# The last three memory key tiles as products of rounded fp32 parts

## The chip, the cores and the metric

The kernel runs on one core of a Trainium2 chip. The core has a matrix engine (PE, with its weight loads shown as PEld), a vector engine (DVE), a scalar engine (ACT), GpSimd (POOL) and a queue that issues transfers (SP). Each engine works off its own instructions in the order in which they were written. The metric is the device time of one execution in microseconds (us); the profile describes one such execution.

## The reference

One step of a decoder layer over 1024 prompt tokens and 8 new tokens, model width 1024. It begins, as far as this change goes, with the keys and values of 256 memory tokens:

```python
def rms_norm(x, g):
    xf = x.astype(jnp.float32)
    y = xf * lax.rsqrt(jnp.mean(xf * xf, axis=-1, keepdims=True) + EPS)
    return (y * g.astype(jnp.float32)).astype(x.dtype)

def memory_kv(mem, g, w_mk, w_mv):
    m = rms_norm(mem, g)
    k = jnp.einsum('bmd,de->bme', m, w_mk)      # 256 x 1024, an output
    v = jnp.einsum('bmd,de->bme', m, w_mv)      # 256 x 1024, an output
...
h = rms_norm(x, g_mix)
z = jnp.einsum('btd,de->bte', h, w_in)          # the first dense products
```

Behind it come a short convolution, an indexer with top-k, sparse attention, attention over the memory and a feed-forward block, which this change doesn't touch.

## The kernel before

Activations lie transposed in SBUF: x is eight tiles `xs[k]` of 128 channels by 1032 tokens, the memory is two tiles `mg[a]` that hold four groups of 128 channels by 256 tokens each. A product of high accuracy is made from parts: a value is split into a rounded high part (ACT, `AF.Copy` to the type fp32r) and a rest (DVE or POOL, a subtraction), and PE computes high x high, high x low and low x high. Weights arrive as units of 128x1024 (`W`): `load_to` issues the transfer on SP, `split_to` splits a unit (ACT at L163, the subtraction on DVE here, L165), `take(8)` hands out the eight blocks of a split unit after making sure that the next ones are loaded and split, and `take_raw` hands out an unsplit unit.

The first 70 us run in program order, with no scheduler:

- Loads are issued in a row on SP: memory and unit 0, then units 1 and 2, x0 and x1, unit 3, x2 and x3, unit 4, x4 and x5, unit 5, x6 and x7, then units 6 to 10.
- Units 0 to 7 are the memory key weights, one for each of the eight key tiles `j`. A key tile is eight products of 128x256 in plain fp32, of `w` and `mg` (L733); the trace shows two records for each product. DVE evicts tile `j` at L708 (`evict_mk`).
- Between the tiles stands the norm of x: ACT squares the tiles x0 to x7 (L697, at j = 1 to 5) and DVE adds them up into `xacc` (L703, one round later). After tile 6, PE sums `xacc` over the partitions (`rstd_sum`, L442), DVE and ACT make the inverse root and a diagonal of it (`rstd_chain`, L446 to L454), and unit 8 is split. After tile 7, PE spreads the root over all rows (`rstd_rows`, L461), copied out at L462.
- Units 8 to 15 are the memory value weights (L781), made from parts. Beside each unit DVE also scales one tile of x (`xnorm`, L719) and subtracts for its split (`split_sb`, L502; the copy on ACT is L499).
- Then the dense products over x begin (L480, `dense`), whose first weight is unit 16.

Buffers come from a ring of 49 slots (`S.get`, `S.put`), oldest first.

Of the kernel before, what the change touches and what calls it, by code (L numbers as in the profile page):

```python
# [110 lines left out]


MIX_UNITS = 24
PE_STEP = "pe"


# [82 lines left out]
class UnitWeights:  # L199


    def __init__(self, nc, slots, ws):
        self.nc, self.slots, self.ws = nc, slots, ws
        self.n = MIX_UNITS
        self.raw, self.hl = {}, {}
# [61 lines left out]
class Background:  # L267
# [15 lines left out]
    def step(self, g):  # L283
        try:
# [3 lines left out]
            return None  # L288
        if c == PE_STEP:
            self.blocked.append(g)  # L290
# [34 lines left out]
def build(tc, A):  # L325
# [15 lines left out]
    PS = psum.tile([128, 8, 512], F32, name="PS")  # L341
    S = Slots(main)
    W = Weights(nc, S, A["ws"])
    W.limit = 21
    bg = Background()
    V, ACT, G, PE = nc.vector, nc.scalar, nc.gpsimd, nc.tensor
    later = []

    def flush():
        for f in later:  # L350
            f()
        later.clear()
# [25 lines left out]
    def load_mem(a, hf):  # L378
        c = slice(512 * hf, 512 * hf + 512)
        nc.sync.dma_start(memr[a][0][:, c], A["memT"][:, 4 * a + 2 * hf:4 * a + 2 * hf + 2, :].rearrange("p k m -> p (k m)"))  # L380
# [8 lines left out]
    for hf in range(2):  # L389
        c = slice(512 * hf, 512 * hf + 512)  # L390
        load_mem(0, hf)
        nc.sync.dma_start(w0[0][:, c], A["ws"][0][:, c])
    W.loaded, W.split = 1, 8
    load_mem(1, 0)
    load_mem(1, 1)
    for w, x in ((3, 2), (4, 4), (5, 6), (6, 8)):
# [43 lines left out]
    def rstd_sum(sq, gp, ng):  # L440
        for g in range(ng):
            PE.matmul(PS[0:gp, 6, g:g + 1], sq[:, g * gp:(g + 1) * gp], ones[:, 0:1], start=True, stop=True)  # L442

    def rstd_chain(gp, ng, src=None):
        v, r, t = sv[0:gp, 0:ng], sr[0:gp, 0:ng], stt[0:gp, 0:ng]
        V.tensor_scalar(v, PS[0:gp, 6, 0:ng] if src is None else src, 1.0 / 1024, EPS, op0=ALU.mult, op1=ALU.add)  # L446
        ACT.activation(t, v, AF.Sqrt)
        V.reciprocal(r, t)
        V.tensor_tensor(t, r, r, op=ALU.mult)
        V.scalar_tensor_tensor(t, t, -0.5, v, op0=ALU.mult, op1=ALU.mult)  # L450
        V.scalar_tensor_tensor(r, t, 1.5, r, op0=ALU.add, op1=ALU.mult)
        dg = S.get()
        d = dg[0][0:gp, 0:ng * gp].rearrange("p (g n) -> p g n", n=gp)
        V.tensor_tensor(d, ident[0:gp, 0:gp].unsqueeze(1).to_broadcast([gp, ng, gp]),  # L454
                        r.unsqueeze(2).to_broadcast([gp, ng, gp]), op=ALU.mult)
        return dg

    def rstd_rows(dg, gp, dst, width, chunk):
        for i, c in enumerate(range(0, width, chunk)):
            b = 6 + i % 2  # L460
            PE.matmul(PS[:, b, :chunk], ones[0:gp, :], dg[0][0:gp, c:c + chunk], start=True, stop=True)  # L461
            (V.tensor_copy if i % 2 == 0 else ACT.copy)(dst[:, c:c + chunk], PS[:, b, :chunk])  # L462
        S.put(dg)
# [33 lines left out]
    def split_sb(src, scale=None, lo=None, width=T):  # L497
        h, l = S.get(F32R), S.get(F32R)
        ACT.activation(h[0][:, :width], src[0][:, :width], AF.Copy, scale=1.0 if scale is None else scale)  # L499
        hf = h[0].bitcast(F32)[:, :width]  # L500
        if scale is None:
            (lo or G).tensor_tensor(l[0][:, :width], src[0][:, :width], hf, op=ALU.subtract)  # L502
        else:
            V.scalar_tensor_tensor(l[0][:, :width], src[0][:, :width], scale, hf, op0=ALU.mult, op1=ALU.subtract)
        return h, l
# [172 lines left out]
    mg = [S.get(), S.get()]  # L678
    W.lo_engines = [V]
    for k in range(8):  # L680
        a, c = k // 4, (k % 4) * 256
# [13 lines left out]
    def x_square(k):  # L695
        xsq[k] = S.get()
        ACT.activation(xsq[k][0][:, :T], xs[k][0][:, :T], AF.Square)  # L697

    def x_accum(k):
        if k == 0:  # L700
            xacc[0] = xsq[0]
        else:
            V.tensor_tensor(xacc[0][0][:, :T], xacc[0][0][:, :T], xsq[k][0][:, :T], op=ALU.add)  # L703
            S.put(xsq[k])

    def evict_mk(j):
        dst = mstage[j // 4][0][:, (j % 4) * 256:(j % 4) * 256 + 256]
        V.tensor_tensor(dst, PS[:, j % 6, :256], mR[0][:, :256], op=ALU.mult)  # L708
        if j % 4 == 3:
            a = j // 4  # L710
            store(mkT[4 * a:4 * a + 4].rearrange("k p m -> p k m"),
                  mstage[a][0][:, :1024].rearrange("p (k m) -> p k m", m=256), mstage[a])

    dgm = dgx = None
    mh, ml = [], []
# [6 lines left out]
        h.append(split_sb(xs[k], lo=V))  # L722

    for j in range(8):
        w = W.take_raw()
        flush()
        if j == 0:
            for a in range(2):
                ACT.activation(msq[a][0][:, :1024], memr[a][0][:, :1024], AF.Square)
                S.put(memr[a])  # L730
        for k in range(8):
            a, c = k // 4, (k % 4) * 256
            PE.matmul(PS[:, j % 6, :256], w[0][:, 128 * k:128 * k + 128], mg[a][0][:, c:c + 256], start=k == 0, stop=k == 7)  # L733
        S.put(w)
        if j == 0:
            V.tensor_tensor(msq[0][0][:, :1024], msq[0][0][:, :1024], msq[1][0][:, :1024], op=ALU.add)
            V.tensor_tensor(msq[0][0][:, :512], msq[0][0][:, :512], msq[0][0][:, 512:1024], op=ALU.add)
            V.tensor_tensor(msq[0][0][:, :256], msq[0][0][:, :256], msq[0][0][:, 256:512], op=ALU.add)
            S.put(msq[1])
        if j == 1:  # L740
            rstd_sum(msq[0][0], 128, 2)
            dgm = rstd_chain(128, 2)
            V.tensor_copy(mrs, sr[:, 0:2])
            S.put(msq[0])
        if j == 2:
            rstd_rows(dgm, 128, mR[0], 256, 256)
            for a in range(2):
                hl = split_sb(mg[a], lo=V, width=1024)
                mh.append(hl[0])
                ml.append(hl[1])  # L750
        for k in X_SQUARE.get(j, ()):
            x_square(k)
        for k in X_SQUARE.get(j - 1, ()):
            x_accum(k)
        if j >= 2:
            for q in ([0, 1, 2] if j == 2 else [j]):
                evict_mk(q)
        if j == 6:
            rstd_sum(xacc[0][0], 86, 12)
            dgx = rstd_chain(86, 12)  # L760
            S.put(xacc[0])
            xR = S.get()
            W.split_to(9)
        if j == 7:
            rstd_rows(dgx, 86, xR[0], T, CH)
    for t in mg:
# [2 lines left out]
    for hv in range(2):  # L769
        for kp in range(4):  # L770
            blocks = W.take(8)
            flush()
            u = W.cur - 1
            for p in range(3):
                for kk in range(2):
                    k = 2 * kp + kk
                    a, c = k // 4, (k % 4) * 256
                    x = ml if p == 1 else mh
                    w = (W.L if p == 2 else W.H)[u][0][:, kk * 512:kk * 512 + 512]
                    for m in range(2):  # L780
                        PE.matmul(PS[:, 2 - 2 * hv + m, :], x[a][0][:, c + 128 * m:c + 128 * m + 128], w,  # L781
                                  start=(k == 0 and p == 0), stop=(k == 7 and p == 2))
# [88 lines left out]
    for n, t in enumerate((7, 6, 5, 4, 3, 2, 1, 0, 8)):  # L871
        c0 = NS + 128 * t if t < 8 else 0
        b = n % 6
        for k in range(8):
# [3 lines left out]
            for p, (x, w) in enumerate(((hh, wh), (hl, wh), (hh, wl))):  # L878
                PE.matmul(PS[:, b, :260], x[0][:, c0:c0 + 128], w[0][:, ws], start=(k == 0 and p == 0),
                          stop=(k == 7 and p == 2))  # L880
# [621 lines left out]
    mg = []  # L1502
# [111 lines left out]
    def mem_sample(hd):  # L1614
# [4 lines left out]
        for x in range(2):  # L1619
            V.tensor_copy(rep[:, 128 * x:128 * x + 128].rearrange("p (b r) -> p b r", r=16),  # L1620
                          qm_s[:, 2 * hd + x, :].unsqueeze(2).to_broadcast([128, NS, 16]))
        yield PE_STEP
        for x in range(2):
# [13 lines left out]
        yield None  # L1637
        yield PE_STEP
        PE.matmul(P, sel128, p, start=True, stop=True)
# [6 lines left out]
        yield None  # L1646
        yield PE_STEP
        for x in range(2):
# [215 lines left out]
    UW.n = A["wu"].shape[0]  # L1864
    UW.load(MIX_UNITS)
    for f in FF_DIRECT:
# [10 lines left out]
        if f == 0:  # L1877
            UW.sums(MIX_UNITS)
            UW.high(MIX_UNITS, "U")
            UW.low(MIX_UNITS, "U")  # L1880
        else:
            UW.high(MIX_UNITS, "V")
            UW.low(MIX_UNITS, "V")
# [92 lines left out]
    blocks = W.take(8 * n)  # L1976
# [72 lines left out]
    for c, cn in enumerate(CW):  # L2049
# [8 lines left out]
        for o in seq:  # L2058
# [5 lines left out]
            if prev is not None:  # L2064
# [4 lines left out]
                if o >= FIN_AT + 2:  # L2069
                    z = o - FIN_AT - 2  # L2070
                    w = 6 - FIN_AT
# [92 lines left out]
```

## Time and profile before

| | |
|---|---|
| median of three runs | 2075.16 us (2074.70 to 2077.28) |
| the profiled execution | 2075.18 us, of which the span is 2073.4 us |
| PE busy | 2037.3 us, 98% of the span |
| DVE busy | 1236.9 us, 60% |
| ACT busy | 821.6 us, 40% |
| POOL busy | 402.5 us, 19% |

A busy share is an average over the span. For a change in one stage, the timeline of that stage tells more: a row gives the start of a group of like instructions, its length, the line and the operands, and in brackets how long the engine had been idle before it and which instruction it waited for. A row without brackets followed the one before it without a wait.

### The profile page before, as it was taken

The page shows a single profiled execution, that of the slowest core. Times are in us where ns is not written, and L with a number is a line of the kernel's source. Part 1 is how long each engine was busy: PE and PEld are TensorE (multiplying, and loading weights), DVE is VectorE, ACT ScalarE, POOL GpSimd, SP SyncE. Part 2 cuts the span into 40 slices and gives each one's busy share as a digit, 9 for nine tenths or more (in the row PEclk, how much of TensorE's full clock was granted, in tenths as well). Part 3 has the DMA queues.
Part 4 walks back from the last instruction along what each step waited for, and adds up shares of the span by engine and source line. Part 5 has one row for each costly group of instructions (what it writes and reads, how often), then busy time and mean ns, then how long its engine had stood idle before and what let it go on. Part 6 is the DMA issues. An engine that isn't in the chain of part 4 may idle for free. (4 is left out here: it accounts for less than half of the span.)

```text
span 2073.4 us, 35037 instructions
## 1 busy us (share of the span) xinstructions
PE 2037.3 (98%) x14455; PEld 1972.7 (95%) x14455; DVE 1236.9 (60%) x2174; ACT 821.6 (40%) x1326; POOL 402.5 (19%) x307
## 2 busy tenths in 40 slices
PE   8999999999999999999999999999999999999998
PEld 7999999999999987889999989999999999999997
DVE  6757677779866346852234787467677677721114
ACT  4437667775324235751122252343222222321204
POOL 0000000000001233333434352420000000274404
PEclk9999999999999999999999999999999999999999
DMA  7212312121327540053324424312221321453102
GB/s 297 87 42 83 123 42 82 62 82 52 135 93 265 179 141 29 1 194 94 131 92 148 181 101 164 116 38 73 85 78 62 103 82 62 166 192 103 51 1 82
DMA packets 79873, 217.48 MB, mean 105 GB/s; under 512 B 9690, under 2 KB 24354, under 8 KB 79714
## 3 DMA queue, kind: packets, MB, share of 16 engines
q1 hardware_dynamic: 79170, 214.73, 29.6%
q8 instruction: 113, 1.85, 0.4%
q10 hardware_dynamic: 544, 0.53, 0.1%
q14 instruction: 46, 0.38, 0.1%
HBM read 167.28 MB, written 47.94 MB: 104 GB/s over the span
## 5 line engine op out<-in xcount | busy, mean ns | idle before, releaser
L610 PE MATMUL PS<-t,t 128*128 128x258 f32 x7392 | 893.8, 283 | 7.3 <-DVE t L1887 3.2
L610 PEld LDWEIGHTS PS<-t,t 128*128 128x128 f32 x7392 | 890.8, 189 | 10.2 <-DVE t L1887 3.4
L480 PE MATMUL PS<-t,t 128*128 128x344 f32 x4824 | 769.1, 320 | 3.1 <-DVE t L165 1.3
L480 PEld LDWEIGHTS PS<-t,t 128*128 128x128 f32 x4824 | 760.7, 188 | 7.1 <-issue 1.7
L165 POOL TENSOR_TENSOR t<-t,t 128x1024 fp32r<-128x1024 f32 x66 | 160.8, 2446 | 354.9 <-ACT t L163 326.5
L251 DVE TENSOR_TENSOR t<-t,t 128x1024 fp32r<-128x1024 f32 (+1 forms) x176 | 188.8, 1086 | 6.4 <-ACT t L238 6.4
L238 ACT ACTIVATE t<-t 128x1024 fp32r<-128x1024 f32 (+1 forms) x176 | 161.7, 947 | 68.8 <-DVE t L228 60.8
L948 ACT ACTIVATE PS<-t,cand 128x1024 f32<-128x1024 f32 (+4 forms) x160 | 144.0, 900 | 55.6 <-DVE cand L955 52.5
L1967 DVE TENSOR_TENSOR t<-PS,t 128x1032 f32<-128x1032 f32 x32 | 39.5, 1233 | 163.1 <-PE PS L480 163.1
L531 POOL TENSOR_TENSOR t<-t,t 128x1032 fp32r<-128x1032 f32 x22 | 53.7, 2454 | 416.1 <-ACT t L530 401.5
L662 DVE TENSOR_TENSOR t<-t,t 128x1032 f32<-128x1032 f32 (+1 forms) x100 | 114.0, 1149 | 2.8 <-ACT t L1873 2.3
L163 ACT ACTIVATE t<-t 128x1024 fp32r<-128x1024 f32 x79 | 82.3, 1051 | 72.8 <-PE PS L480 60.9
L616 DVE TENSOR_TENSOR t<-PS,t 128x516 f32<-128x516 f32 x44 | 30.6, 695 | 108.8 <-PE PS L610 108.1
L499 ACT ACTIVATE t<-t 128x1032 fp32r<-128x1032 f32 (+2 forms) x34 | 36.0, 1067 | 142.2 <-DVE t L1511 77.1
L614 ACT COPY t<-PS 128x516 f32<-128x516 f32 x44 | 25.9, 589 | 164.8 <-PE PS L610 164.6
L1528 DVE TENSOR_TENSOR t<-PS,t 128x1032 f32<-128x1032 f32 x32 | 39.4, 1232 | 79.6 <-PE PS L480 79.6
L1599 DVE CUSTOM_DVE_ANT_0 caus<-t,t 128x256 bf16<-128x256 f32 x128 | 78.7, 615 | 10.3 <-ACT t L1641 5.3
L502 POOL TENSOR_TENSOR t<-t,t 128x1032 fp32r<-128x1032 f32 (+1 forms) x22 | 53.5, 2438 | 109.4 <-ACT t L499 91.5
L619 ACT COPY t<-PS 128x516 f32<-128x516 f32 x26 | 15.4, 592 | 144.5 <-PE PS L610 144.5
L1220 POOL TENSOR_SCALAR t<-t,ast 128x128 f32<-128x128 f32 (+7 forms) x64 | 48.1, 752 | 120.2 <-DVE ast L1219 88.0
L530 ACT ACTIVATE t<-t 128x1032 fp32r<-128x1032 f32 x40 | 41.4, 1060 | 74.1 <-PE PS L480 46.8
L1239 DVE TENSOR_TENSOR t<-PS,t 128x512 fp32r<-128x512 f32 x72 | 49.6, 688 | 32.1 <-ACT t L1235 31.4
(269 smaller groups left out, 2017.5 us busy)
## 6 DMA issues: line engine op xcount, KB each, us to landing
t<-in_ws_dram SPq DMA_DIRECT2D x86, 512.0 KB, 4.9
t<-in_wu_dram SPq DMA_DIRECT2D x44, 512.0 KB, 4.1
t<-in_wu_dram SPq DMA_DIRECT2D x88, 256.0 KB, 5.4
fd<-t SPq DMA_DIRECT2D x18, 516.0 KB
t<-fd SPq DMA_DIRECT2D x18, 516.0 KB, 11.5
t<-in_xT_dram SPq DMA_DIRECT2D x16, 516.0 KB, 8.1
t<-in_cmk_dram SPq DMA_DIRECT2D x16, 512.0 KB, 5.4
t<-in_cmv_dram SPq DMA_DIRECT2D x16, 512.0 KB, 6.0
```

What stands on the lines that cost most here:

```text
L163: nc.scalar.activation(h[0][:, :1024], raw[0][:, :1024], AF.Copy)
L165: eng.tensor_tensor(l[0][:, :1024], raw[0][:, :1024], h[0].bitcast(F32)[:, :1024], op=ALU.subtract)
L238: self.nc.scalar.activation(h[0][:, :w], self.raw[u][x][0][:, :w], AF.Copy)
L251: self.nc.vector.tensor_tensor(l[0][:, o:o + w], raw[0][:, :w], h[0].bitcast(F32)[:, :w], op=ALU.subtract)
L480: PE.matmul(PS[:, b + c, :CH], w, x[0][:, c * CH:(c + 1) * CH], start=(k == 0 and p == 0), stop=(k == n - 1 and p == 2))
L502: (lo or G).tensor_tensor(l[0][:, :width], src[0][:, :width], hf, op=ALU.subtract)
L531: lo.tensor_tensor(l[0][:, a:b], raw[0][:, a:b], h[0].bitcast(F32)[:, a:b], op=ALU.subtract)
L610: PE.matmul(PS[:, banks[z] + c, :HC], a, b[:, HC * c:HC * c + HC], start=j < 3 and q == 0 and p == 0 or j == 5 and q == 0 and p == 0, stop ...
L662: V.tensor_tensor(o, o, i, op=ALU.mult)
L948: ACT.activation(wide[:, :128 * (i + 1)], sc[i], AF.Sign, bias=candf[:, n:n + 1], scale=-1.0, accum_out=tval[:, n:n + 1])
L1239: V.tensor_tensor(tl[0][:, :512], PS[:, t_bank(x), :], th[0].bitcast(F32)[:, :512], op=ALU.subtract)
L1599: V.tensor_tensor_reduce(out=caus, in0=s[0][:, 256 * x:256 * x + 256], in1=rows, scale=1.0, scalar=0.0, op0=ALU.mult, op1=ALU.add, accum_o ...
```

## The change

The weight units 5, 6 and 7 are split like the later ones, and key tiles 5, 6 and 7 are computed as three products of parts: 24 products of 128x256 in fp32r in place of eight in fp32. The parts of the memory (`mh`, `ml`) were already made at j = 2 for the values. Unit 5 is split at j = 3; `take(8)` then splits unit 6 at j = 5, unit 7 at j = 6 and unit 8 at j = 7, so the call that split unit 8 at j = 6 is gone.

```diff
+MK_RAW = 5
...
-    W.loaded, W.split = 1, 8
+    W.loaded, W.split = 1, MK_RAW
...
     for j in range(8):
-        w = W.take_raw()
+        if j < MK_RAW:
+            w = W.take_raw()
+        else:
+            blocks = W.take(8)
...
+            if j < MK_RAW:
+                PE.matmul(PS[:, j % 6, :256], w[0][:, 128 * k:128 * k + 128], mg[a][0][:, c], start=k == 0, stop=k == 7)
+            else:
+                for p, (y, x) in enumerate(((0, mh), (0, ml), (1, mh))):
+                    PE.matmul(PS[:, j % 6, :256], blocks[k][y], x[a][0][:, c], start=k == 0 and p == 0,
+                              stop=k == 7 and p == 2)
...
+        if j == 3:
+            W.split_to(MK_RAW + 1)
...
             xR = S.get()
-            W.split_to(9)
```

In the changed file lines are shifted (L165 is L166, L703 is L704, L708 is L709, L697 is L698, L446 is L447).

DVE before, from the eviction of key tiles 0 to 2 to the last row ahead of the root chain. `t_212` is the accumulator, `t_178` and `t_179` the staged key tiles:

```order
L708 TENSOR_TENSOR t_178<-PS,t_176 128x256 x3
L703 TENSOR_TENSOR t_212<-t_212,t_232 128x1032
L708 TENSOR_TENSOR t_178<-PS,t_176 128x256
L703 TENSOR_TENSOR t_212<-t_212,t_245 128x1032
L703 TENSOR_TENSOR t_212<-t_212,t_247 128x1032
L708 TENSOR_TENSOR t_179<-PS,t_176 128x256
L703 TENSOR_TENSOR t_212<-t_212,t_260 128x1032
L703 TENSOR_TENSOR t_212<-t_212,t_262 128x1032
L708 TENSOR_TENSOR t_179<-PS,t_176 128x256
L703 TENSOR_TENSOR t_212<-t_212,t_275 128x1032
L703 TENSOR_TENSOR t_212<-t_212,t_277 128x1032
L708 TENSOR_TENSOR t_179<-PS,t_176 128x256
```

The same place on DVE now, without its first and its last row; `t_107`, `t_113` and `t_115` are the units 5, 6 and 7:

```order
L166 TENSOR_TENSOR t_246<-t_107,t_245 128x1024
L704 TENSOR_TENSOR t_212<-t_212,t_232 128x1032
L709 TENSOR_TENSOR t_178<-PS,t_176 128x256
L704 TENSOR_TENSOR t_212<-t_212,t_249 128x1032
L704 TENSOR_TENSOR t_212<-t_212,t_251 128x1032
L709 TENSOR_TENSOR t_179<-PS,t_176 128x256
L166 TENSOR_TENSOR t_272<-t_113,t_271 128x1024
L704 TENSOR_TENSOR t_212<-t_212,t_264 128x1032
L704 TENSOR_TENSOR t_212<-t_212,t_266 128x1032
L709 TENSOR_TENSOR t_179<-PS,t_176 128x256
L166 TENSOR_TENSOR t_307<-t_115,t_306 128x1024
L704 TENSOR_TENSOR t_212<-t_212,t_299 128x1032
```

Three subtractions have come in: one ahead of the first accumulation, one ahead of the fourth and one ahead of the sixth.

ACT before, from the square of x1 (`t_93`) to the root and the copy of unit 8:

```order
L697 ACTIVATE t_232<-t_93 128x1032
L697 ACTIVATE t_245<-t_97 128x1032
L697 ACTIVATE t_247<-t_99 128x1032
L697 ACTIVATE t_260<-t_103 128x1032
L697 ACTIVATE t_262<-t_105 128x1032
L697 ACTIVATE t_275<-t_109 128x1032
L697 ACTIVATE t_277<-t_111 128x1032
L447 ACTIVATE stt<-sv 86x12
L163 ACTIVATE t_314<-t_117 128x1024
```

ACT now:

```order
L698 ACTIVATE t_232<-t_93 128x1032
L164 ACTIVATE t_245<-t_107 128x1024
L698 ACTIVATE t_249<-t_97 128x1032
L698 ACTIVATE t_251<-t_99 128x1032
L698 ACTIVATE t_264<-t_103 128x1032
L698 ACTIVATE t_266<-t_105 128x1032
L164 ACTIVATE t_271<-t_113 128x1024
L698 ACTIVATE t_299<-t_109 128x1032
L698 ACTIVATE t_301<-t_111 128x1032
L164 ACTIVATE t_306<-t_115 128x1024
L448 ACTIVATE stt<-sv 86x12
L164 ACTIVATE t_360<-t_117 128x1024
```

The copies of units 5, 6 and 7 stand among the squares, that of unit 5 right behind the square of x1. Unit 8's copy (`t_117`) keeps its place behind the root.

## Rows read from the trace of the kernel before

**Rows 1.** The page: span, and PE's busy time, share and instructions.
```profile
span 2073.4 us, 35037 instructions
...
PE 2037.3 (98%) x14455; PEld 1972.7 (95%) x14455; DVE 1236.9 (60%) x2174; ACT 821.6 (40%) x1326; POOL 402.5 (19%) x307
```

**Rows 2.** Timeline of PE, 12 to 70 us: start, length, work [idle before, releaser].
```profile
19.86 13.98 PE L733 MATMUL PS<-t,t 128*128 128x256 f32 x64
33.68 1.93 PE L442 MATMUL PS<-ones,t 128*86 128x1 f32 x24
35.47 3.70 PE L733 MATMUL PS<-t,t 128*128 128x256 f32 x16
39.01 2.20 PE L461 MATMUL PS<-t,ones 86*128 86x344 f32 x6
40.78 21.75 PE L781 MATMUL PS<-t,t 128*128 128x512 f32 x92
...
66.32 3.90 PE L480 MATMUL PS<-t,t 128*128 128x344 f32 x23 [1.34 <-DVE t L165]
```

**Rows 3.** Timeline of DVE, 10 to 46 us: accumulations of squares, root chain.
```profile
23.67 1.22 DVE L703 TENSOR_TENSOR t<-t,t 128x1032 f32<-128x1032 f32 x1
...
30.77 2.56 DVE L703 TENSOR_TENSOR t<-t,t 128x1032 f32<-128x1032 f32 x2
...
35.64 0.17 DVE L446 TENSOR_SCALAR sv<-PS 86x12 f32<-86x12 f32 x1 [1.34 <-PE PS L442]
```

**Rows 4.** Timeline of DVE, 38 to 66 us.
```profile
38.10 1.22 DVE L165 TENSOR_TENSOR t<-t,t 128x1024 fp32r<-128x1024 f32 x1
39.24 0.41 DVE L708 TENSOR_TENSOR t<-PS,t 128x256 f32<-128x256 f32 x1
39.78 0.52 DVE L462 COPY t<-PS 128x344 f32<-128x344 f32 x1
41.24 0.52 DVE L462 COPY t<-PS 128x344 f32<-128x344 f32 x1 [0.94 <-PE PS L461]
41.80 1.23 DVE L165 TENSOR_TENSOR t<-t,t 128x1024 fp32r<-128x1024 f32 x1
...
65.05 1.21 DVE L165 TENSOR_TENSOR t<-t,t 128x1024 fp32r<-128x1024 f32 x1
```

**Rows 5.** Timeline of PE, 1223 us: 24 products of 128x256.
```profile
1223.38 3.05 PE L1684 MATMUL PS<-t,t 128*128 128x256 f32 x24
```

**Rows 6.** The page's costliest groups: line, form, count | busy, mean ns | idle.
```profile
L163 ACT ACTIVATE t<-t 128x1024 fp32r<-128x1024 f32 x79 | 82.3, 1051 | 72.8 <-PE PS L480 60.9
```

**Rows 7.** Timeline of ACT, 19 to 28 us: the squares of x1 to x7.
```profile
19.22 4.86 ACT L697 ACTIVATE t<-t 128x1032 f32<-128x1032 f32 x5
25.15 1.07 ACT L697 ACTIVATE t<-t 128x1032 f32<-128x1032 f32 x1 [1.06 <-DMA t<-in_xT_dram]
26.43 1.07 ACT L697 ACTIVATE t<-t 128x1032 f32<-128x1032 f32 x1 [0.22 <-DMA t<-in_xT_dram]
```

**Rows 8.** Timeline of SP's queue, 13 to 17 us: loads as they are issued.
```profile
13.68 0.33 SPq L151 DMA_DIRECT2D t<-in_ws_dram  x1
14.97 1.61 SPq L385 DMA_DIRECT2D t<-in_xT_dram  x2
```

**Rows 9.** Timeline of PE: its three longest waits behind 100 us.
```profile
169.90 0.39 PE L610 MATMUL PS<-t,t 128*128 128x258 f32 x1 [2.16 <-ACT t L908]
...
1191.51 7.47 PE L1684 MATMUL PS<-t,t 128*128 128x256 f32 x48 [2.15 <-ACT t L1641]
...
1405.89 14.32 PE L610 MATMUL PS<-t,t 128*128 128x258 f32 x117 [3.22 <-DVE t L1887]
```

**Rows 10.** Stretches: busy us of engines (instructions), granted clock, DMA share, GB/s.
```profile
core 0: us, PE busy (x) PEld busy (x) DVE busy (x) ACT busy (x) POOL busy (x), PEclk, DMA share, GB/s
1192.00:1196.00 4.00, 4.00 (x24) 4.00 (x23) 3.83 (x11) 0.00 (x0) 1.78 (x1) 0.57 0.39 128
168.00:172.00 4.00, 2.10 (x17) 2.10 (x18) 3.29 (x6) 4.00 (x7) 0.00 (x0) 1.00 0.33 132
1404.00:1408.00 4.00, 2.11 (x17) 2.12 (x18) 4.00 (x7) 2.44 (x5) 0.00 (x0) 1.00 0.35 124
```

More of the change, by code (lines that the diff above doesn't have):

```diff
@@ L731, in build @@
         for k in range(8):
-            a, c = k // 4, (k % 4) * 256
-            PE.matmul(PS[:, j % 6, :256], w[0][:, 128 * k:128 * k + 128], mg[a][0][:, c:c + 256], start=k == 0, stop=k == 7)
-        S.put(w)
+            a, c = k // 4, slice((k % 4) * 256, (k % 4) * 256 + 256)
+            if j < MK_RAW:
[4 more added lines that the diff above has]
+                              stop=k == 7 and p == 2)
+        if j < MK_RAW:
+            S.put(w)
+        else:
+            W.close()
+        if j == 3:
+            W.split_to(MK_RAW + 1)
         if j == 0:
```

## The prediction

> **What bounds the kernel now.** The page says that PE is busy for 98% of the span [rows 1], so one would cost this edit in PE time alone. But the share is an average, and the edit sits in the first 40 us, so I read that stretch engine by engine, and then the place where it hands over to the long dense products.
>
> The first reading is PE against DVE around the sum of squares of x. PE computes tiles 3 to 6 in one run of 64 records from 19.86 and starts the sum over partitions (L442) at 33.68 [rows 2]. On DVE the seven accumulations of squares start at 23.67, and the last two start at 30.77 and end at 33.33 [rows 3]. Between them stand only the small evictions of key tiles (L708); DVE has no gap. So L442 finds its two inputs ready within 0.4 us of each other: PE in its order, and DVE's sum. Here both are late, and whatever is added to either one moves L442.
>
> The second reading is what follows L442. DVE waits for it until 35.64 [rows 3], does the root chain, builds a diagonal and works off the splits and norms. From 41.80 on, 21 rows stand back to back; the last of them, at 65.05, is the low part of the first dense weight and ends at 66.26 [rows 4]. PE meanwhile does tile 7, the rows product L461 and the memory values L781, and then waits 1.34 us for just that DVE row, until 66.32 [rows 2]. So from 41.80 to 66.3 DVE sets the pace, not PE, and behind 66.3 the dense products run on without a gap. A shift of DVE at 41.80 is a shift of the dense products and so, I take it, of the end.
>
> **The change part by part.** All times are in the profiled execution of 2075.18 us, whose median of three runs is 2075.16, so no correction is needed between the two.
>
> PE work: a key tile in fp32 takes 16 of the 64 records, 13.98 / 4 = 3.5 us [rows 2]. The new tile has 24 products of 128x256 between rounded parts. The trace has the same shape and count in L1684, 3.05 us [rows 5]. The saving is about 0.45 us a tile, 1.4 us for three, if PE were the bound. [...]
>
> Split work: units 5, 6 and 7 now each need a copy on ACT (L163, 1.05 us [rows 6]) and a subtraction on DVE (L165, which holds DVE for 39.24 - 38.10 = 1.14 us [rows 4]). The order listing shows where: all three subtractions stand ahead of the last two accumulations, one ahead of the first. Unit 8 is split where it was, behind the root chain. So DVE has 3 x 1.14 = 3.4 us more in a queue without a gap, all of it ahead of L442.
>
> A wait: unit 5's copy stands on ACT behind the square of x1 and ahead of the squares of x2 to x7. In the kernel before, ACT runs from 19.22 through five squares without stopping, then waits until 25.15 and 26.43 for the last two tiles of x [rows 7]; these land 1.28 us apart. On SP, the load of unit 5 was issued at 13.68, just ahead of that of x6 at 14.97 [rows 8]; the distance of issue is the distance of landing, so unit 5 lands at 25.15 - 1.29 = 23.86. ACT's copy therefore runs from about 23.9 to 24.95, with the squares held up behind it, and DVE, which reached the first accumulation at 23.67, waits 1.3 us for it. The squares that follow do not hold DVE up again: x2 and x3 are ready by about 27.0, and DVE comes to them at 27.6 and 28.8; unit 6 lands at 27.7 (behind x7), is copied by 29.8, and DVE comes to its subtraction at 30.4; x6, x7 and unit 7 are likewise done by 32.8, ahead of DVE.
>
> Sum to L442: 1.3 + 3.4 = 4.7 us. Less 0.1 us, the slack that DVE's sum had against PE's own queue: L442 starts 4.6 us later, at about 38.2.
>
> Behind L442: tile 7 is 0.45 us shorter, so the rows product L461 starts that much sooner against the chain. In the kernel before DVE was free about 0.2 us before its first copy of these rows (39.24 plus 0.34 for an eviction is 39.58, and the copy started at 39.78), and that is all it can gain; the second copy at 41.24 follows the first [rows 4]. So -0.2. At 41.80, and so at 66.3 and at the end, DVE is 4.4 us late. The PE saving of tiles 5 and 6 is worth nothing, since PE then only waits longer for L442.
>
> TensorE's clock: PE is now idle twice. It ends tile 4 at 26.9 as before and tile 5 at about 29.9, and waits 1.7 us for unit 6's low part (30.4 + 1.2); it ends tile 6 at about 34.5 and waits 3.7 us for the accumulations, until 38.2. No row shows exactly that. [...] Its price from the same rows: 48 products of L1684 took 7.47 us there against 2 x 3.05 = 6.10, a loss of 1.4 us [rows 5, 9]. Here L442 and tile 7 come first, and both stand between the accumulations and DVE's copies, so I take the whole 1.4 us. Bounds: 0 if the clock falls inside the wait and recovers, or not at all; 1.9 (L442 at half rate throughout, its 24 records last 1.93 now [rows 2]) plus about 1 of tile 7, so 2.9 at most. [...]
>
> Sum: 2075.18 + 4.4 + 1.4 = 2081.0 us.
>
> Other edits at nothing: the loads of units 11 and 12 keep their place on SP, between the two stores of keys; POOL has nothing to do with this stage; ACT's three copies cost nothing beyond the wait above, as ACT has nothing between 27.5 and the root chain behind L442 [rows 3, 7]. Slots turn over by the same rule; I read no dense load that waits for one more here.
>
> **The rivals.**
> - Full clock: all as above without a fall, 2075.18 + 4.4 = 2079.6. For it speaks the 3.22 us wait that did not lower the clock [rows 9, 10].
> [...]
> - The other side, faster: the dense start is PE's and not DVE's. If DVE catches up its 4.4 us between 41.80 and 66.3, the end moves by PE's work alone, 3 x 0.45 = 1.4 us, to 2073.8. It decides if the row at 65.05 ended more than 1.34 us earlier, for then PE would not have waited [rows 2, 4]. Against it: no gap in DVE's rows over which to catch up. [...]
>
> **How the numbers follow.** Clock falls: 0.50, 2081.0, own range 2079.8 to 2082.6. Full clock: 0.25, 2079.6. No wait on ACT: 0.17, 2078.3. Faster side: 0.04, 2073.8. Something else: 0.04. Runs of before spread over 2.6 us, so each case is blurred by about a microsecond. The range goes from 2077.8 to 2082.9: the case of no ACT wait lies just inside, the faster side and the tail of a doubled clock loss are left out. A measurement can tell 0.2%, 4.15 us, so slower means above 2079.3: nearly all of the first case (0.45), over half of the second (0.14) and a little of the rest (0.03), 0.62. Faster than 2071 has 0.02; the rest, 0.36, is no change.
>
> **What would show each step.** In the trace after: an ACT copy of unit 5 that starts at about 23.9 behind a wait for the load; three DVE subtractions between 24.9 and 35.6; the last accumulation ending near 38.0, and L442 right behind it; PE waits of about 1.7 and 3.7 us; a granted clock below 1 between 36 and 43; the first dense run starting near 72 (70.7 without the fall). The forecast is wrong if L442 starts before 36, if DVE shows gaps behind 46, or if PE's waits later in the program shrink by what was lost here.

## The result, and the profile after

The changed kernel took 2090.13 us (median, 2089.63 to 2091.74) against 2076.17 us (2074.70 to 2077.28) for the kernel before on the same chip: a ratio of 1.0066, 95% interval 1.0054 to 1.0078. That is slower by 14 us. The forecast was 2081.0, in a range up to 2082.9: right in sign, far too small in size, and outside its range. The profiled execution took 2090.09 us, against 2075.18 before; the traces of these two are compared below.

The page of the changed kernel, answering [rows 1, 6]: span and instructions, busy time by engine, ACT's copies of weights. Lines behind L114 have moved: L163, L165 are now L164, L166; L442, L461, L480 are L443, L462, L481; L703, L708 are L704, L709; three-product tiles are L741.

```profile
span 2088.0 us, 35090 instructions
...
PE 2042.0 (98%) x14479; PEld 1977.3 (95%) x14479; DVE 1241.8 (59%) x2177; ACT 823.7 (39%) x1329; POOL 402.3 (19%) x307
...
L164 ACT ACTIVATE t<-t 128x1024 fp32r<-128x1024 f32 x82 | 85.4, 1050 | 77.0 <-PE PS L481 60.8
```

PE has 24 more products, ACT three more copies and DVE three more subtractions, as the change intends. PE's share is 98% as before, and tells nothing. The first stage, up to the dense products, tells more. PE, 25 to 74 us (start, length, work [idle before, releaser]), for [rows 2]:

```profile
25.38 3.19 PE L741 MATMUL PS<-t,t 128*128 128x256 f32 x24
28.75 0.50 PE L741 MATMUL PS<-t,t 128*128 128x256 f32 x2 [0.19 <-ACT t L164]
30.67 2.85 PE L741 MATMUL PS<-t,t 128*128 128x256 f32 x22 [1.42 <-DVE t L166]
36.96 3.68 PE L443 MATMUL PS<-ones,t 128*86 128x1 f32 x24 [3.43 <-DVE t L704]
40.49 5.47 PE L741 MATMUL PS<-t,t 128*128 128x256 f32 x24
45.76 2.54 PE L462 MATMUL PS<-t,ones 86*128 86x344 f32 x6
...
73.42 33.40 PE L481 MATMUL PS<-t,t 128*128 128x344 f32 x210 [1.35 <-DVE t L166]
```

DVE in the same stretch, for [rows 3, 4], and ACT, for [rows 7]:

```profile
23.97 1.23 DVE L166 TENSOR_TENSOR t<-t,t 128x1024 fp32r<-128x1024 f32 x1 [1.42 <-ACT t L164]
...
29.40 1.22 DVE L166 TENSOR_TENSOR t<-t,t 128x1024 fp32r<-128x1024 f32 x1
...
33.28 1.22 DVE L166 TENSOR_TENSOR t<-t,t 128x1024 fp32r<-128x1024 f32 x1
34.41 2.49 DVE L704 TENSOR_TENSOR t<-t,t 128x1032 f32<-128x1032 f32 x2
...
40.67 0.17 DVE L447 TENSOR_SCALAR sv<-PS 86x12 f32<-86x12 f32 x1 [3.43 <-PE PS L443]
...
72.15 1.22 DVE L166 TENSOR_TENSOR t<-t,t 128x1024 fp32r<-128x1024 f32 x1
```

```profile
22.88 1.06 ACT L164 ACTIVATE t<-t 128x1024 fp32r<-128x1024 f32 x1 [3.82 <-DMA t<-in_ws_dram]
23.84 3.91 ACT L698 ACTIVATE t<-t 128x1032 f32<-128x1032 f32 x4
```

ACT waits for the load of unit 5, DVE waits 1.42 us for ACT's copy, the three subtractions stand in DVE's queue ahead of the last accumulations, and L443 waits for those. So far it went as forecast. But L443 took 3.68 us instead of 1.93, and tile 7 took 5.47 us where 24 products took 2.85 to 3.19 just before. The stretches of the changed kernel (busy us of PE, PEld, DVE, ACT, POOL with instructions, granted clock, DMA share, GB/s) show why; 1192 and 1404 answer [rows 10]:

```profile
36.00:38.00 2.00, 1.04 (x7) 1.04 (x8) 1.24 (x2) 0.00 (x0) 0.00 (x0) 0.55 0.01 2
38.00:46.00 8.00, 8.00 (x43) 8.00 (x44) 3.26 (x7) 1.16 (x2) 0.00 (x0) 0.50 0.00 0
46.00:48.00 2.00, 1.97 (x7) 0.98 (x6) 0.94 (x2) 0.54 (x2) 0.00 (x0) 0.89 0.30 102
...
1192.00:1196.00 4.00, 4.00 (x24) 3.45 (x23) 3.90 (x8) 1.06 (x1) 2.83 (x2) 1.00 0.91 360
1404.00:1408.00 4.00, 4.00 (x27) 4.00 (x26) 2.98 (x3) 1.42 (x3) 0.00 (x0) 1.00 0.01 4
1418.00:1422.00 4.00, 3.92 (x20) 3.92 (x21) 4.00 (x7) 0.63 (x2) 0.00 (x0) 0.58 0.71 231
```

The granted clock was 0.50 for 10.2 us, from 36.2 to 46.5, though PE was busy from 36.96 on. The other falls in the two traces, the program's end left out, are to 0.50 too and last 3.4 us each (at 1192.6 before, at 1138.7 and 1418.6 after).

The second reading is where the loss grew. For the same DVE instruction in two traces, its start minus its start in the kernel before is the shift at that place. This table is worked out from DVE's timelines: us by which a kernel is later, at places named by the time in the kernel before (the labels are those of the experiments). A column is one execution, the profiled one: for x3_dve_only and x5_delay it was the slowest of its kernel, for x2_late_split and x11_half_packet the fastest.

```
at us   after  x1_filler  x2_late  x3_dve  x5_delay  x6_pad  x11_half  x12_half
   20   -1.20      -0.50    -0.37    0.10     10.24   -0.81     -0.98      0.05
   66    7.10       3.84     5.99    7.50     10.23   -0.82      5.18      0.04
  250    7.09       5.30     6.06    8.97     11.76    0.70      6.63      1.67
  512    7.06       5.48     6.00    8.81     11.76    0.62      6.70      1.69
  565   10.07       6.30     9.23    8.72     11.74    2.99      6.62      1.77
 1100    9.70       5.91     8.87   10.21     13.21    4.52      6.27      1.66
 1150   13.50       5.94     8.92    9.06     13.17    4.53     10.08      1.68
 1203   11.86       5.87     7.42    7.59     13.22    4.52      8.44      0.17
 1440   13.68       5.90     9.62   12.29     14.71    4.48     10.25      1.79
 2050   14.65       6.83    10.05   12.94     14.72    4.48     11.18      1.79
```

Half of the loss, 7.1 us, is there at the dense start (66). The rest comes at a few places far behind code that the change touches: +3.0 between 512 and 565, +3.8 between 1100 and 1150, and a step of about 1.5 wherever the clock falls (to 0.50) for 3.4 us in one kernel and not in the other: the kernel before has such a fall at 1192 [rows 9, 10] that the changed one lacks (-1.6 at 1203), and the changed one has one at 1418.

The place at 512: ACT's copies (first row: kernel before, second: changed kernel), then the DMA engines' busy share in 40 slices of 0.1 us, from 512.5 before and from 519.5 after. The store of cvd, 516 KB from SBUF to HBM, is issued at 512.61 and at 519.67.

```profile
515.32 1.06 ACT L238 ACTIVATE t<-t 128x1024 fp32r<-128x1024 f32 x1 [2.92 <-DVE cand L969]
```

```profile
524.25 1.06 ACT L239 ACTIVATE t<-t 128x1024 fp32r<-128x1024 f32 x1 [4.80 <-DMA cvd<-t]
```

```profile
DMA  0000000007999899999998100000000000000060
```

```profile
DMA  0000000001997998979979600200010011011010
```

Before, the store's bytes move in one block of 1.43 us, and a lone packet of 0.02 MB (the 6 near the end, of kind "instruction", queue q8) follows 1.4 us later; I take it for a piece of the program that is fetched. After, this packet falls into the store (it begins 0.94 us behind the issue, the store's bytes 0.83), and the store's bytes take 3.19 us, the last of them in a thin trickle. ACT, whose copy cannot begin before the store has left its buffer, waits until 524.25, and the conversions, products and stores behind it are late too. All fourteen traces, those of the experiments below included, divide in this way: the store's bytes take 1.43 to 1.44 us in the six where no such packet begins between 6.4 us ahead of the issue and 3.4 behind it, and 2.2 to 3.5 us in the eight where one begins 0.4 to 1.7 us behind it.

### The profile page after: what moved, and what is told of

It is laid out like the page before. It is cut to its first block, busy times and chain, and to the rows that moved or that the text cites. A ratio compares the mean times of both kernels' runs of the same rounds, so it can differ in the third digit from the quotient of the medians.

```text
span 2088.0 us, 35090 instructions
## 1 busy us (share of the span) xinstructions
PE 2042.0 (98%) x14479; PEld 1977.3 (95%) x14479; DVE 1241.8 (59%) x2177; ACT 823.7 (39%) x1329; POOL 402.3 (19%) x307
## 3 DMA queue, kind: packets, MB, share of 16 engines
q8 instruction: 113, 1.85, 0.4%
## 5 line engine op out<-in xcount | busy, mean ns | idle before, releaser
L481 PE MATMUL PS<-t,t 128*128 128x344 f32 x4824 | 770.8, 321 | 3.2 <-DVE t L166 1.3
L481 PEld LDWEIGHTS PS<-t,t 128*128 128x128 f32 x4824 | 762.5, 188 | 7.1 <-issue 1.7
L166 POOL TENSOR_TENSOR t<-t,t 128x1024 fp32r<-128x1024 f32 x66 | 160.9, 2444 | 358.1 <-ACT t L164 330.5
L164 ACT ACTIVATE t<-t 128x1024 fp32r<-128x1024 f32 x82 | 85.4, 1050 | 77.0 <-PE PS L481 60.8
```

Of the source, the lines that this page charges most:

```text
L164: nc.scalar.activation(h[0][:, :1024], raw[0][:, :1024], AF.Copy)
L166: eng.tensor_tensor(l[0][:, :1024], raw[0][:, :1024], h[0].bitcast(F32)[:, :1024], op=ALU.subtract)
L481: PE.matmul(PS[:, b + c, :CH], w, x[0][:, c * CH:(c + 1) * CH], start=(k == 0 and p == 0), stop=(k == n - 1 and p == 2))
```

## The experiments

My theory after the result: the split work delays L443 by 4.5 us as forecast; the clock then costs near 4 us, not 1.4; and a longer stream of PE's instructions moves the fetch onto the store. The rival for the first stage was that three-product tiles or SP's order lose the time themselves; the rival for the later places, that lateness alone costs more further on.

**x0_again**, the changed kernel once more, unchanged.

> The changed kernel once more, for a second trace of it. What stands in both traces is the kernel's, what stands in one is that execution's. Theory, the code load: the wait of ACT for a stored tile near 524 us (4.80 us there) comes again, and the shift against before grows by 2 to 3 us between 512 and 565 us again. The falls of the clock behind 1100 us may sit elsewhere; each moves the shift by about 1.5 us.

2091.86 us (2091.76 to 2092.01), ratio 1.0070 (1.0055 to 1.0086). Shifts: 7.62 at 66, 10.32 at 565, 15.13 at 1150, 16.07 at 2050; the wait for the store was 5.12 us. The pattern belongs to the kernel, not to one execution.

**x1_filler**: work for PE while it waits for the accumulations.

```diff
+            for i in range(14):
+                PE.matmul(PS[:, 7, :], mh[0][0][:, 0:128], mh[0][0][:, 0:512], start=True, stop=True)
```

> The changed kernel, with 14 products of 128x512 between parts of the memory put on PE ahead of the sum L443 (into a bank that is written anew later), where PE waited 3.43 us. Theory, the clock: with PE at work in that wait the granted clock stays at 1.00 from 36 to 46 us; L443 takes 1.9 us again in place of 3.68 and key tile 7 about 3.0 in place of 5.47, so the first dense run starts some 3.5 us earlier, near 70 against 73.42, and the time falls from 2090.1 to about 2086.5. Rival, the wait and not the clock is the cost: the dense start stays at 73.4 (within 0.5 us) and the time at 2090.

2084.49 us (2081.30 to 2086.99), ratio 1.0039 (1.0026 to 1.0052). PE of x1_filler, and the clock:

```profile
37.82 2.00 PE L443 MATMUL PS<-ones,t 128*86 128x1 f32 x24 [0.20 <-DVE t L704]
39.68 3.07 PE L741 MATMUL PS<-t,t 128*128 128x256 f32 x24
```

```profile
38.00:46.00 8.00, 7.57 (x59) 6.44 (x59) 4.89 (x12) 3.22 (x5) 0.00 (x0) 1.00 0.15 49
```

With the wait filled, the granted clock stays at 1.00, L443 is back at 2.00 us and tile 7 at 3.07, and the shift at 66 is 3.84 instead of 7.10. Counted from the first sum of squares (row 20 of the table), it is 4.34 instead of 8.30. L443 still starts late, so the split work stays, and what is gone is the clock. These rows show that the clock stayed up here, where PE had work in place of the wait (7.57 of 8.00 us); in the changed kernel, once it had fallen, 8.00 us of work from 38 to 46 did not bring it back (0.50). The median is 2 us below the 2086.5 that were expected: this trace loses 0.8 us at the store and nothing at 1100, where the changed kernel loses 3.0 and 3.8.

**x2_late_split**: unit 5 split one tile later, so that ACT does not hold the squares up behind its load.

```diff
-        if j == 3:
+        if j == 4:
             W.split_to(MK_RAW + 1)
```

> The changed kernel, with unit 5 split at j = 4 in place of j = 3, so that its copy on ACT stands behind the squares of x2 and x3. Theory: ACT no longer holds the squares up while unit 5 is on its way, DVE loses its 1.42 us wait ahead of the first subtraction, and L443 starts 1.3 us earlier against the first tiles; if the clock still falls, the time is 1.3 us less, near 2088.8. Rival: the squares behind unit 5's copy were what DVE would have waited for anyway, and nothing moves (2090.1).

2086.99 us (2085.88 to 2091.63), ratio 1.0058 (1.0041 to 1.0075). L443 starts 21.05 us behind the first sum of squares (L443 at 14.33 in the changed kernel), against 22.63: 1.6 us earlier, so the wait on ACT was worth at least the 1.3 us of the forecast.

**x3_dve_only**: the kernel before, with the three copies and subtractions alone; their results are read by nothing, and the tiles stay in fp32.

```diff
+    def copy_only(u):
+        r, hx, lx = W.raw[u], S.get(F32R), S.get(F32R)
+        ACT.activation(hx[0][:, :1024], r[0][:, :1024], AF.Copy)
+        V.tensor_tensor(lx[0][:, :1024], r[0][:, :1024], hx[0].bitcast(F32)[:, :1024], op=ALU.subtract)
+        extra.extend((hx, lx))
...
+        if j in (5, 6):
+            copy_only(j + 1)
...
+        if j == 3:
+            copy_only(5)
...
-    for t in mg:
+    for t in mg + extra:
```

> The kernel before, with the three copies on ACT and the three subtractions on DVE at the places where the changed kernel has them, into buffers that nothing reads; the key tiles stay in fp32. Theory, the split work is the loss: DVE's last accumulation ends 4.6 us later against the first tiles, PE waits some 3 us for it, the clock falls, and the dense products start at least as late as in the changed kernel (7 us later than before, or more, as tile 7 in fp32 at half clock takes 7 us). Rival, the three products themselves cost the time: the dense products start within 1 us of before. On the 7.5 us that the changed kernel lost behind the dense start (2007.1 us from there to the end of the span before, 2014.6 after): if the late start itself brings them, they come here too and the time is about 2090; if PE's other instructions bring them, the time is 2083 to 2085.

2085.44 us (2082.68 to 2088.36), ratio 1.0038 (1.0023 to 1.0052). PE of x3_dve_only:

```profile
37.77 2.73 PE L442 MATMUL PS<-ones,t 128*86 128x1 f32 x24 [3.83 <-DVE t L703]
40.36 6.31 PE L743 MATMUL PS<-t,t 128*128 128x256 f32 x16
...
73.83 6.39 PE L480 MATMUL PS<-t,t 128*128 128x344 f32 x39 [1.35 <-DVE t L165]
```

Nearly the whole loss of the first stage is here without one three-product tile: L442 waits 3.83 us, the clock falls, and the dense start shifts by 7.5 us. Counted from the first sum of squares that is 7.4, against 8.3 in the changed kernel, whose fall of the clock was longer (10.2 us against 6.8). So the loss needs no three-product tile, and what these tiles cost or save in this stage is within 0.9 us. But between 512 and 565 this kernel, as late as the changed one, loses nothing (8.81 to 8.72). So lateness is not what costs 3 us there. The median lies next to the 2083 to 2085 that were expected if PE's other instructions bring the later loss.

**x5_delay**: the kernel before, all of it later by a copy from HBM to HBM at the head of SP's queue.

```diff
+    scratch = dram.tile([6, 128, 1024], F32, name="scratch")
+    nc.sync.dma_start(scratch, A["ws"][0:6])
```

> The kernel before with one transfer of 3 MB between two places in HBM put ahead of the first loads on SP's queue, so that everything starts later by some 8 to 16 us and nothing else is changed; the delay is read from the start of the first key tile. Theory, a shift of the whole program moves what meets in time (transfers, clock) and costs something of its own: the time from the dense start to the end differs from 2007.1 by 3 us or more. Rival: it stays within 2 us of 2007.1, and the 7.5 us of the changed kernel come from its instructions, not from its lateness.

2087.80 us (2086.59 to 2090.35), ratio 1.0052 (1.0036 to 1.0069). In the profiled execution, the one of 2090.35, the dense start shifts by 10.24 and the end by 14.7. The 4.5 us on top are three more falls of the clock (at 181, 778 and 1420 us, 1.5 each); between 512 and 565 nothing is lost. But two of the four executions, 2086.59 and 2086.78, are 10.3 and 10.5 us above the kernel before (2076.33), about the shift of the dense start and no more. So the theory held in one execution and the rival in two: lateness alone cost 4.5 us further on in the one and nothing in the others. Behind the waits of 2.16 and 3.22 us the clock stayed at 1.00 in the kernel before [rows 9, 10]; behind the same two it was 0.50 here, from 181 and from 1420. Each of the three falls moved what followed by 1.5 us.

**x6_pe_pad**: the kernel before, with 24 small products in the 1.34 us in which PE waits for DVE [rows 2].

```diff
+    for i in range(24):
+        PE.matmul(PS[0:32, 7, 0:64], mh[0][0][:, 0:32], mh[0][0][:, 0:64], start=True, stop=True)
```

> The kernel before, with 24 small products (32 columns of weights, 64 moving columns, into a bank that is free there) put on PE ahead of the first dense product, where PE waited for DVE anyway; so PE's stream is 48 instructions longer, as in the changed kernel, and the stage before it is not. Theory, the longer stream moves the load of code into the store near 512 us: the dense start stays within 0.5 us of before, and the shift grows by 2 to 3 us between 512 and 565 us, with a wait of ACT for the stored tile; the time is 2078 to 2080. Rival, that wait comes from the lateness or from the new slots: no such wait, the time stays at 2076.3.

2079.16 us (2077.41 to 2081.04, ten runs), ratio 1.0012 (1.0002 to 1.0021). The dense start is not later (-0.8), and yet the wait for the store is there and 2.4 us are lost between 512 and 565:

```profile
517.53 1.06 ACT L238 ACTIVATE t<-t 128x1024 fp32r<-128x1024 f32 x1 [4.51 <-DMA cvd<-t]
```

Nothing in this kernel is moved; PE's stream is longer by 24 products, as many as the change adds. In the kernels whose stream is as long as before (x3_dve_only, x5_delay, x7_pool_low) the packet comes 3.4 to 3.6 us behind the issue of the store, and no such wait is seen.

**x4_pool**: the change, split late, with the subtractions of units 5 to 7 on POOL.

```diff
+    W.lo_engines = [V if u < MK_RAW or u > 7 else G for u in range(W.n)]
...
-        if j == 3:
+        if j == 4:
```

> The changed kernel, with unit 5 split at j = 4 and the subtractions of units 5, 6 and 7 on POOL in place of DVE. Theory: DVE has neither the wait nor the 3.4 us, so its last accumulation ends where it did before (17.8 us behind the first sum L443, which was 33.33 against 15.53), PE has no wait of 3.4 us, the clock does not fall, and the dense start is within 1 us of before against the first sum. What the changed kernel loses behind 500 us with its longer stream (about 3 us) stays. Time 2077.5 to 2080. Rival, ACT's copies or PE's own form cost the stage its time: the dense start stays 4 us or more late.

2093.59 us (2086.16 to 2096.37; the profiled execution is the lowest), ratio 1.0083 (1.0068 to 1.0099). A miss: L443 still waits, and the dense start shifts by 5.29. DVE and POOL of x4_pool:

```profile
23.93 4.53 DVE L704 TENSOR_TENSOR t<-t,t 128x1032 f32<-128x1032 f32 x2
```

```profile
24.33 3.04 POOL L166 TENSOR_TENSOR t<-t,t 128x1024 fp32r<-128x1024 f32 x1 [21.00 <-ACT t L164]
```

Two accumulations beside one subtraction on POOL take 4.53 us, against 2.56 in [rows 3]: DVE loses 2.0 us to a subtraction that it gave away, where doing it itself costs 1.14. **x7_pool_low** asks the same of the kernel before, for all the splits that DVE does until the dense start:

```diff
-    W.lo_engines = [V]
+    W.lo_engines = [G]
```

> The kernel before, with the subtractions of the weight units 8 to 20 on POOL, which is idle there, in place of DVE. If DVE sets the pace from 41.80 to 66.3, as the prediction has it, then without eight subtractions of 1.14 us there PE's own work is the bound: L781 needs 21.75 us from 40.78, so the dense products start near 63.7 in place of 66.32, 2.6 us sooner, and the time falls to about 2073.7. Rival, POOL's 2.4 us for each is late, or the two engines get in each other's way: the dense start stays or is later, and the time is 2076.3 or more.

2088.61 us (2085.92 to 2090.51), ratio 1.0052 (1.0039 to 1.0066). Another miss. DVE, POOL and PE of x7_pool_low:

```profile
41.85 6.82 DVE L719 SCALAR_TENSOR_TENSOR t<-t,gains,t 128x1032 f32<-128x1032 f32 x2
```

```profile
41.83 12.49 POOL L165 TENSOR_TENSOR t<-t,t 128x1024 fp32r<-128x1024 f32 x4 [1.45 <-ACT t L163]
```

```profile
74.68 5.60 PE L480 MATMUL PS<-t,t 128*128 128x344 f32 x20 [2.37 <-POOL t L165]
```

A norm on DVE takes 6.82 / 2 = 3.4 us beside POOL's subtractions, and 1.28 in the kernel before, where POOL has nothing to do from 38 to 66; a subtraction on POOL takes 12.49 / 4 = 3.1 us, and 2.45 in the mean of the kernel before. The dense products now wait for POOL, 8.4 us later. Both are slower here; what holds them up no run isolates.

**x9_pad_more** and **x10_after_pad** make PE's stream longer still, the first on x6_pe_pad, the second on the changed kernel, to move the fetch away from the store.

```diff
+    for i in range(64):
+        PE.matmul(PS[0:32, 7, 0:16], ones[:, 0:32], ones[:, 0:16], start=True, stop=True)
```

> The kernel before, with the 24 small products of x6_pe_pad and 64 more (one row of 32 by 16, on the constant ones) while PE has nothing to do ahead of the first key tile; nothing reads them. The stream of PE's instructions is longer than in x6_pe_pad by 64 products and their weight loads; no work is moved. Theory (a piece of code that is fetched meets the store of cvd, and the place in time at which it is fetched hangs on the length of PE's stream): the fetch now falls ahead of the store or elsewhere, ACT at L238's place waits 2.9 us for cand as in the kernel before and not 4.5 for the store, the shift between 512 and 565 us is under 1 us instead of 2.4, and the time is 2076 to 2078. Rival (any longer stream, or an idle PE that is made busy, costs these microseconds): the wait of 4.5 us or more stays, and the time is 2079 or more.

> The changed kernel, with the same 64 small products ahead of the first key tile. Theory (meeting of a code fetch with the store): the dense start stays 7 to 8 us late, but the wait of 4.8 us for the store of cvd is gone or moved, the shift does not grow between 512 and 565 us, and the time is about 2087. Rival (the 3 us between 512 and 565 come from the late stage, or from the three-product tiles themselves): the wait stays, and the time is 2090 or more.

2083.84 us (2082.57 to 2086.86), ratio 1.0040 (1.0028 to 1.0053), and 2092.43 us (2091.29 to 2095.27), ratio 1.0081 (1.0065 to 1.0098). The theory's forecast failed in both: 2.0 us are still lost between 512 and 565 in the first, 2.8 in the second, and the packet sits again 0.6 and 0.8 us behind the store's issue. (The 64 products also take 7.0 us, longer than PE's idle time there, so the first tile is 2.4 us late.) The instruction queues on the pages of the kernel before and of x10_after_pad (packets, MB, share) show what I had overlooked:

```profile
q8 instruction: 113, 1.85, 0.4%
```

```profile
q8 instruction: 114, 1.87, 0.4%
```

No row names the engine that these packets are for. My estimate, if they are PE's code: 1.85 MB over the 2 x 14455 records of PE and PEld is 64 bytes each, and 28910 / 113 is 256 instructions a packet. The 64 products are 128 records of matmuls and 128 of weight loads: by that estimate one whole packet (114 for 113), which leaves the later packets where they were against the work. So half a packet was tried, 32 products instead of 64: **x11_half_packet** on the changed kernel, **x12_pad_half** on x6_pe_pad.

```diff
-    for i in range(64):
+    for i in range(32):
```

> As x10_after_pad, with 32 small products instead of 64. Why: the page counts 113 instruction packets of 1.85 MB on q8 in the kernel before, the size of PE's 2 x 14455 instructions at 64 bytes, so a packet is 256 instructions; the 64 products of x10_after_pad were 128 records of matmuls and 128 of weight loads, one whole packet (114 on its page), which leaves every later packet where it was against the work. 32 products are half a packet. Theory (the packet of PE's code meets the store of cvd): the packet now comes some 10 us from the store, ACT waits 2.9 us for cand there and not 4.8 for the store, the shift between 512 and 565 us grows by less than 0.7 instead of 3, and the time is 2087 to 2088. Rival (the 3 us belong to the three-product tiles, to lateness or to any longer stream): wait and jump stay, 2090 or more.

> As x6_pe_pad, with 32 further small products (half a packet of PE's code) while PE has nothing to do ahead of the first key tile; x9_pad_more had 64 there, one whole packet. Theory (packet meets store): the wait of 4.5 us for the store of cvd that x6_pe_pad and x9_pad_more have is gone, ACT waits 2.9 us for cand, the shift between 512 and 565 us grows by under 0.7 instead of 2.4, and the time is 2076 to 2078 plus whatever the products delay the first tile by (under 1 us). Rival: the wait stays in any longer stream, and the time is 2079 or more.

ACT at the place of the store, x11_half_packet and then x12_pad_half:

```profile
522.01 1.06 ACT L239 ACTIVATE t<-t 128x1024 fp32r<-128x1024 f32 x1 [2.92 <-DVE cand L984]
```

```profile
517.00 1.06 ACT L238 ACTIVATE t<-t 128x1024 fp32r<-128x1024 f32 x1 [2.92 <-DVE cand L973]
```

The wait is gone in both, the packets on q8 begin 6.4 us ahead of the store's issue and 10.3 and 9.9 us behind it, and the shift between 512 and 565 goes from 6.70 to 6.62 and from 1.69 to 1.77. x12_pad_half took 2076.57 us (ten runs), ratio 1.0001 (0.9992 to 1.0011), 0.4 us above its runs of the kernel before, where x6_pe_pad, with a shorter stream, was 2.6 above its own. That settles the place at 512 for these traces: the store takes 2.2 to 3.5 us where a packet on q8 begins 0.4 to 1.7 us behind its issue, and 24 or 32 small products on PE move that packet onto the store or away from it. How much a meeting costs is not settled: x1_filler, with its packet 0.4 us behind the issue, lost 0.8 us, x9_pad_more (0.6) 2.0 and the changed kernel (0.9) 3.0. x11_half_packet shows it in its trace (span 2084.7); its median, 2089.85 (2086.76 to 2090.89, the profile being the lowest), is above the 2088 expected and 0.3 below the changed kernel's, so in its time the 3 us do not show; why its other three executions are 3 to 4 us longer is open.

None of these kernels beats the kernel before; x12_pad_half equals it.

## Why the prediction was wrong

*Split work: right.* Three subtractions at 1.14 us and a wait of 1.42 us on DVE (forecast 1.3). L443 started 3.28 us later than in [rows 2]. This execution, though, was 1.2 us early at its first sum of squares, for a reason outside the change (x6_pe_pad has it too, -0.81; x3_dve_only does not, 0.10). Without that it is 4.5, against the 4.6 of the forecast. The slack, put at 0.1, is 0.29 by the rows: 33.68 - 33.33 [rows 2, 3], less the 0.06 by which PE follows DVE's row at 66.3 [rows 2, 4]; 1.42 + 3.4 - 0.29 is 4.5. x2_late_split takes the wait away, and x3_dve_only shows the wait and the split work without the new tiles.

*PE's saving: right, and worth nothing.* At a granted clock of 1.00 the 24 products took 3.07 to 3.19 us against 3.5 (forecast 3.05), and DVE kept the dense start.

*The clock: right that it falls, wrong in its price.* I took 1.4 us from one fall to 0.50 of 3.4 us, behind a wait of 2.15, that met 48 products [rows 9, 10], and called 2.9 the most. That L443 could run at half rate throughout was in the bound (1.9; it lost 3.68 - 1.93 = 1.75). "About 1 of tile 7" was the wrong term: tile 7 lost 5.47 - 3.07 = 2.4, since the clock stayed down for 10 us, and the rows product 0.34. Together that is 4.5 where I had 1.4; less 0.6, tile 7's own shortening, it makes 3.9, and measured the chain behind L443 loses 7.10 - 3.28 = 3.82, against the 1.2 of the forecast. x1_filler gives 3.3 of it back, or 4.0 counted from the first sum of squares. The length of the fall is no constant. With a wait of 3.4 us before L443 it was 10.2 us in the changed kernel, x0_again and x2_late_split, but 6.8 in x10_after_pad, and 6.8 in x3_dve_only with a wait of 3.8; x4_pool, with 2.9, had 3.4, and x11_half_packet, with 2.2, had two falls of 3.4, in tile 6 and in tile 7. What sets it is open.

*"A shift of the dense products and so, I take it, of the end": wrong, and the larger half of the miss.* The forecast of 5.8 at the end was 7.1 already at 66, and 7.5 more came behind it, for which the sum had no term:
- 3.0 at 512 to 565: the fetch on the store, shown by x6_pe_pad and x12_pad_half. "Slots turn over by the same rule" was true and beside the point; the sum had no term for 48 more PE instructions.
- 3.8 at 1100 to 1150. Two copies on DVE are held up while POOL subtracts. Alone, two such copies take 0.36 us, as in the kernel before at 1146 (first row). At 1123 in the kernel before (second row) one of the two takes 2.42 us; in the changed kernel (third row, POOL's row beside it last) both do, 2.2 us more together. PE waited behind them, at 1138 into a fall of the clock (0.50 from 1138.7 for 3.4 us; 1.5 of the 3.8).

```profile
1146.14 0.36 DVE L1620 COPY t<-qm_s 128x128 f32<-128x128 f32 x2
```

```profile
1123.35 2.55 DVE L1620 COPY t<-qm_s 128x128 f32<-128x128 f32 x2
```

```profile
1133.08 4.79 DVE L1633 COPY t<-qm_s 128x128 f32<-128x128 f32 x2
```

```profile
1130.69 4.81 POOL L503 TENSOR_TENSOR t<-t,t 128x1032 fp32r<-128x1032 f32 x2 [8.78 <-ACT t L500]
```

  POOL works beside the copies in both kernels. They start 2.39 us behind POOL's row here and 2.36 before, but 2.39 also in x2_late_split and x4_pool, where one copy alone is slow, so this distance doesn't decide it. Both copies were slow in all four kernels that split unit 5 early and leave PE idle ahead of L443 (the changed one, x0_again, x10_after_pad, x11_half_packet) and in no other. Why is open; no run isolates it.
- Steps of the clock: -1.6 at 1192 and +1.5 near 1411. In x5_delay the traced execution has three such steps, and two others, by their times, have none.
- Some 0.8 more in small steps: -0.4 at 565 to 1100, +0.2 at 1203 to 1230, and 1.0 spread over 1440 to 2050. What they are is open.

*The rivals.* Full clock (2079.6): what x1_filler built, and its shift at 66, 3.84 or 4.34 from the first sum of squares, is near the forecast's 4.4. No wait on ACT (2078.3) fell with the 3.82 us for which ACT's row waits for the load of unit 5; the faster side fell with PE's wait of 1.35 at 73.42, unchanged. The chances put 0.96 on four cases for the first 70 us and no more than the rest on anything behind; that is why the range was too narrow.

## What to carry to other kernels

Where an edit changes the number of PE's instructions, add to the range what a moved packet of the instruction queue can do to a tight store further on (3.0 us here), and test it with a pad of half a packet (32 products here, by the estimate above) rather than explain it by the edit. Bound the price of a fall of the clock by the work that follows the wait, at half rate (0.50) for as long as the longest fall that a trace of the kernel shows (10.2 us here), and fill the wait with work for PE to see what it costs (3.3 us here, or 4.0 counted from the first sum of squares). Where DVE sets the pace of a stage, as here, three more operations in its queue (3 x 1.14 us, and 1.42 of wait) cost more than the products saved on TensorE (0.3 to 0.6 us a tile), and giving them to GpSimd was no way out: the one beside two accumulations cost DVE 2.0 us instead of 1.14.

## What the runs showed of the hardware that was not expected

- In the changed kernel the granted clock stayed at 0.50 for 10.2 us (36.2 to 46.5) while PE did 24 single-column products and then 24 of 256 columns, busy throughout (38 to 46 us: PE 8.00 of 8.00, clock 0.50). Other falls lasted 3.4 us (the kernel before at 1192.6) or 6.8 (x3_dve_only, at L442).
- Queue q8, of kind "instruction", moved 113 packets of 1.85 MB together; 256 instructions of 64 bytes to a packet is an estimate from that and PE's 28910 records. One packet that began 0.94 us behind the issue of a 516 KB store went with 3.19 us for the store's bytes instead of 1.43; ACT, which then waited for the store, started 4.6 us behind its issue instead of 2.7.
- One subtraction on POOL beside two of DVE's accumulations cost DVE 2.0 us (x4_pool: 4.53 against 2.56); back to back on both, an operation took 3.4 us on DVE (1.28 in the kernel before) and 3.1 on POOL (x7_pool_low).
